# A depthwise convolution as 32x32 matrix tiles in place of 128x32 tiles, vector work and trips through DRAM

## The chip, the core and the metric

The kernel runs on one core of a Trainium2 chip. The core has a matrix engine (TensorE, "PE" in the profile; its weight loads are "PEld"), a vector engine (VectorE, "DVE"), an activation engine (ScalarE, "ACT"), a general engine (GpSimd, "POOL") and a queue engine (SyncE, "SP") that issues most DMAs. Each engine works through its own instructions in order and waits on semaphores for the others. Operands lie in SBUF (128 partitions); TensorE writes its sums to PSUM (eight banks of 512 fp32 numbers per partition). The metric is the time of one execution on the device in microseconds (us).

## What is computed

One step of a streaming encoder: a 512-frame prompt and 8 running streams of 16 new frames each, 640 frames of 1024 features. Layer 0 is a convolution module and a SwiGLU feed-forward block; layer 1 is chunked attention and a second feed-forward block. Only the convolution module concerns us:

```python
def conv_module(h, hist, g, w_pw1, b_pw1, w_dw, b_dw, ln_g, ln_b, w_pw2, b_pw2):
    a, gate = jnp.split(rms_norm(h, g) @ w_pw1 + b_pw1, 2, axis=-1)
    glu = a * jax.nn.sigmoid(gate)
    full = jnp.concatenate([hist.astype(glu.dtype), glu], axis=1)
    y = lax.conv_general_dilated(
        full, w_dw[:, None, :].astype(full.dtype), window_strides=(1,), padding="VALID",
        dimension_numbers=("NWC", "WIO", "NWC"), feature_group_count=D_MODEL) + b_dw
    y = jax.nn.silu(layer_norm(y, ln_g, ln_b))
    return h + y @ w_pw2 + b_pw2, full[:, -CONV_HIST:]
```

The convolution is depthwise and causal: each of the 1024 channels has its own filter of 31 taps over time, and 30 frames of history (zeros for the prompt, `cache_conv` for the streams) stand ahead of the new frames. The last 30 rows of `full` are outputs as well.

## The kernel before

Features lie on partitions: 1024 features are eight blocks (c = 0 to 7) of 128. Frames lie along the free dimension: first the 128 stream frames, then the 512 prompt frames, worked on as two groups of 320 (`GS`); group 0 holds all stream frames and the first 192 of the prompt. Every large product is made in three matmuls of high and low parts (`mm3`, lines L170 to L172, and `product`, L367), for which a weight tile is loaded as `raw` and split by ScalarE (`whi`, L150) and VectorE (`wlo`, L154). The two normalizations over features (`rms`, `conv_ln`) use small matmuls for the sums over partitions (L205) and for spreading the result back (L217).

In the convolution module each block c goes through these steps, written as letters in a list `PLAN` that a loop at the end of the module walks through (L817); a scheduler then places the instructions of each step on the engines, with raised priority for those inside `tc.high_priority`:

- W: load and split the block's weights of the first pointwise product, by DMAs on SyncE's queue (L139).
- a, b: the gated product (`glu`) for group 0 and group 1, 48 matmuls each; ScalarE takes the two sums out of PSUM (L596, L599), VectorE multiplies them (L603, the "gate").
- the depthwise convolution, in one of three ways:
  - d (`conv`): on VectorE, one multiply-add per tap (L676) into an accumulator in PSUM. Block 1's prompt and the stream frames of blocks 0, 1 and 2.
  - q (`conv_pool`): products on ScalarE (L686), sums on GpSimd (L689). The prompts of blocks 0 and 2.
  - k, X, Y, G, H: on TensorE, for blocks 3 to 7. The gate writes the frames into `g4` in four rows by time modulo four. That goes out to DRAM (`sc`, L631) and comes back as sixteen planes `x4` (`shift`, L643), in which a partition is one of four time shifts, one of eight channels and one of four time phases. `conv_w` (k, L696) builds 128x32 weight tiles on GpSimd from a table. `conv_pe` (G for group 0, H for group 1, L716) makes 64 matmuls for G and 32 for H, 128 rows by 32 columns each. VectorE adds the bias (`ev`, L721), the result goes out to DRAM (`ys`, L726) and back (L728) to be rearranged into `y`, and VectorE adds the three taps that the table does not hold, in three to six instructions (L739).
- n (`conv_ln`): LayerNorm and silu for one group, when `y` of all eight blocks is there. `LNO` is the order in which it takes up the blocks.
- w (`pw2`): the second pointwise product for one group, added to the residual `h` (L779).

PSUM before: the sums of products have four banks (`mm`), and the statistics and the VectorE convolution two tiles of two banks each (`w2`).

The order around the change is the list:

```python
LNO = ((0, 1, 3, 4, 5, 2, 6, 7), (0, 1, 2, 3, 4, 6, 7, 5))
PLAN = ("a0 y x1 b0 b1 q0 W2 W3 a2 b2 dp1s0 k3 a3 W4 b3 X3 q2 ds1s2 k4 a4 G3 k5 W5 b4 X4 a5 G4 k6 W6 a6 W7 a7 "
        "G5 Y7 k7 b6 W5 G6 k3 b7 W8 G7 n0 k4 H3 X6 k6 H4 X7 k7 b5 H6 X5 k5 H7 H5 s0 n1 w0 w1")
```

Of the kernel before, what the change touches and what calls it, by code (L numbers as in the profile page):

```python
# [15 lines left out]
P = 128  # L16
D = 1024
# [32 lines left out]
CVT = 4  # L50
C0, NC4 = 3, KT - 3
SG4 = SEG // 4 + 1
NS4, NP4 = NB * SG4, (HIST + T + 2) // 4
L4 = NS4 + NP4
KS, KA, KG = NB * SB // 4, 48, 80
WG, WH = NS4 + KA + 7, KG + 7
# [17 lines left out]
V_B4 = V_DW4 + NC4 * 128  # L74
# [4 lines left out]
def tile_trunk(ctx, tc, xT, vecs, hist, hist4, w_pw1, w_pw2, w_in0, w_out0, w_in1, w_out1,  # L79
# [7 lines left out]
    w2 = early.enter_context(tc.tile_pool(name="w2", bufs=2, space=PSUM))  # L87
# [4 lines left out]
    mm = tps.enter_context(tc.tile_pool(name="mm0", bufs=4, space=PSUM))  # L92
# [9 lines left out]
    def w2t():  # L102
        return w2.tile([P, 1024], F32, tag="w2", name=nm("w2"))
# [24 lines left out]
    def wsplit(src, k, n, parts=1, pool=0, cuts=1, gains=None):  # L128
# [6 lines left out]
        else:  # L135
            src = src if len(src.shape) == 2 else src.rearrange("p m c -> p (m c)")
            for i in range(cuts):
                a, b = sz * i // cuts, sz * (i + 1) // cuts
                nc.sync.dma_start(raw[:, a:b], src[:, a:b])  # L139
# [46 lines left out]
    def colmean(st, pieces, n, cut, tag, eng=nc.gpsimd, accp=None):  # L186
        nt = len(tiles(n))
        srcs = []
# [13 lines left out]
        for k, f in enumerate(srcs):  # L202
            s = f()
            for t, a in enumerate(tiles(n)):
                nc.tensor.matmul(st[:, 512 + t * w + k:513 + t * w + k], s[:, a:a + P],  # L205
                                 onec, start=True, stop=True)
        r = tp.tile([P, 4], F32, tag=tag, name=nm(tag))
        if w > 1:
            nc.vector.tensor_reduce(out=r[:, :nt],
                                    in_=st[:, 512:512 + nt * w].rearrange("p (t k) -> p t k", k=w),  # L210
                                    op=ALU.add, axis=mybir.AxisListType.X)
            return r, r[:, :nt]
        return r, st[:, 512:512 + nt]
# [329 lines left out]
    def load_hist(c0, c1):  # L543
        for c in range(c0, c1):
            if c < C0:
                nc.sync.dma_start(gs[:, c], hist[:, c])
            else:
                nc.sync.dma_start(g4[:, c - C0, :, 0:NS4], hist4[:, c - C0])
# [9 lines left out]
    g4 = cp.tile([P, NC4, 4, L4], F32, name="g4", tag="g4")  # L558
    for i in range(NC4):
        nc.gpsimd.memset(g4[:, i, :, NS4:NS4 + 8], 0.0)  # L560
        nc.gpsimd.memset(g4[:, i, 2:4, L4 - 1:L4], 0.0)
# [18 lines left out]
    def w4t():  # L580
        return cp.tile([P, 1024], F32, tag="w4", name=nm("w4"), bufs=2)

    def glu(c, g, wh, wl, mid=None):
# [10 lines left out]
        with tc.high_priority(offset=HP):  # L594
# [11 lines left out]
            ns = 0 if g else NB * SB  # L606
            o = HIST + g * NH - NB * SB * g
            if c < C0:
                if g == 0:
# [23 lines left out]
        if g == 0:  # L633
            if c < 7:
                shift(c, 0)
# [641 lines left out]
```

## Time and profile before

| | us |
|---|---|
| median of 3 runs | 1575.44 (1565.17 to 1576.24) |
| the profiled execution, its own time | 1576.21 |
| span of that execution in the trace | 1574.4 |
| TensorE busy in the span | 1473.0 (94%) |
| VectorE busy | 1019.5 (65%) |
| ScalarE busy | 671.0 (43%) |
| GpSimd busy | 241.4 (15%) |

All times below are microseconds from the start of the span unless they say ns. The convolution module and the entry to the feed-forward block take the first 307 us; the first pointwise product starts at 17.7, the first LayerNorm's sums are complete at 201.5, and the second pointwise product starts at 225.4. A line of a list of groups gives the source line, engine, operation, output and inputs, shapes and count, then busy us, mean ns of one, and the idle time of the engine ahead of them with what ended it. A line of a timeline gives start, length, and count; in brackets the idle time before it. "PEclk" or a number below 1 after the busy times is the share of full clock speed that TensorE was granted.

### The profile page before, as it was taken

Reading aid. Unit: us, or ns where it says so; the run is one execution under the profiler, and the core shown is the slowest. Engines: PE = TensorE matmul, PEld = TensorE weight load, DVE = VectorE, ACT = ScalarE, POOL = GpSimd, SP = SyncE. Lnnn points to the kernel's source line nnn. Section 1 sums busy time; section 2 is a strip of 40 time slices with the busy share of each in tenths; the row PEclk is TensorE's granted clock in tenths of the full one; section 3 lists DMA queues with packets and bytes.
Section 4 is the critical chain, followed back from the end, with each engine's and each line's share of the span. In section 5 each row is a group of like instructions: output and inputs, shape, how many; then the busy total and the mean of one; then the engine's idle time right before and its main releaser. Section 6 shows DMA issues by size and latency. Waiting matters only on the chain.

```text
span 1574.4 us, 27608 instructions
## 1 busy us (share of the span) xinstructions
PE 1473.0 (94%) x11282; PEld 1414.4 (90%) x11282; DVE 1019.5 (65%) x2020; ACT 671.0 (43%) x1281; POOL 241.4 (15%) x297
## 2 busy tenths in 40 slices
PE   5977668999999999999999999997999999999997
PEld 5977668999999999999988788975999999999996
DVE  6777565785666566658675767563694665575555
ACT  4663334453244244246554444443453254244233
POOL 4876622100000000003221112011000000000001
PEclk9988769899999999999999999997999999999998
DMA  7279653402222223213655445352112213222211
GB/s 236 75 157 190 142 103 107 134 27 81 81 81 89 81 72 108 81 54 99 218 170 192 155 160 201 122 189 67 55 48 88 81 58 105 81 74 88 81 54 67
DMA packets 89183, 171.29 MB, mean 109 GB/s; under 512 B 35552, under 2 KB 60128, under 8 KB 80224
## 3 DMA queue, kind: packets, MB, share of 16 engines
q1 hardware_dynamic: 88768, 169.01, 35.0%
q8 instruction: 88, 1.44, 0.4%
q10 hardware_dynamic: 288, 0.51, 0.1%
q14 instruction: 39, 0.32, 0.1%
HBM read 155.89 MB, written 13.62 MB: 108 GB/s over the span
## 4 chain that ended last, share of the span: by engine, by line
PE 78%; DVE 9%; DMA 6%; ACT 2%; POOL 2%; issue 2%; SPq 1%; POOLq 0%; DVEq 0%; ACTq 0%
PE mm L367 35%; PE mm L170 12%; PE mm L171 12%; PE mm L172 12%; DMA cache<-in_ck 2%; DVE wlo L154 1%; DMA ys<-ev 1%; PE w L1057 1%; DVE w L676 1%; PE am L1042 1%; DMA sc<-g 1%; POOL ca L689 1%; PE am L1025 1%; DVE g L603 1%; PE am L1088 1%
## 5 line engine op out<-in xcount | busy, mean ns | idle before, releaser
L367 PE MATMUL mm<-XH,wlo 128*128 128x320 f32 x736 | 228.8, 311 | 0.8 <-DVE wlo L325 0.8
L367 PE MATMUL mm<-XH,whi 128*128 128x320 f32 x736 | 227.5, 311 | 0.0
L367 PE MATMUL mm<-XL,whi 128*128 128x320 f32 x736 | 225.2, 309 | 0.0
L170 PE MATMUL mm<-xh,whi 128*128 128x320 f32 (+2 forms) x640 | 204.9, 323 | 11.3 <-ACT xh L159 5.3
L171 PE MATMUL mm<-xh,wlo 128*128 128x320 f32 (+2 forms) x640 | 203.7, 320 | 1.1 <-DVE wlo L154 1.1
L172 PE MATMUL mm<-xl,whi 128*128 128x320 f32 (+2 forms) x640 | 199.0, 317 | 0.4 <-DVE xl L160 0.4
L171 PE MATMUL mm<-hid,wlo 128*128 128x320 f32 (+2 forms) x560 | 171.8, 308 | 0.0
L172 PE MATMUL mm<-hid,whi 128*128 128x320 f32 (+2 forms) x560 | 169.3, 308 | 0.0
L170 PE MATMUL mm<-hid,whi 128*128 128x320 f32 (+2 forms) x560 | 167.7, 308 | 0.0
L324 ACT ACTIVATE whi<-raw 128x1536 fp32r<-128x1536 f32 (+2 forms) x90 | 100.9, 1149 | 119.6 <-PE mm L172 87.9
L325 DVE TENSOR_TENSOR wlo<-raw,whi 128x1536 fp32r<-128x1536 f32 (+2 forms) x90 | 118.6, 1342 | 39.9 <-ACT whi L324 39.8
L367 PEld LDWEIGHTS mm<-XH,wlo 128*128 128x128 f32 x736 | 139.2, 189 | 1.6 <-DVE wlo L325 1.6
L367 PEld LDWEIGHTS mm<-XH,whi 128*128 128x128 f32 x736 | 138.9, 189 | 0.0
L170 PEld LDWEIGHTS mm<-xh,whi 128*128 128x128 f32 x640 | 124.9, 196 | 14.8 <-ACT xh L159 6.4
L367 PEld LDWEIGHTS mm<-XL,whi 128*128 128x128 f32 x736 | 138.0, 188 | 0.0
L171 PEld LDWEIGHTS mm<-xh,wlo 128*128 128x128 f32 x640 | 125.4, 196 | 2.1 <-DVE wlo L154 1.6
L172 PEld LDWEIGHTS mm<-xl,whi 128*128 128x128 f32 x640 | 123.4, 194 | 1.9 <-issue 1.0
L367 PE MATMUL mm<-XH,vhi 128*128 128x320 f32 x368 | 114.7, 312 | 0.0
L367 PE MATMUL mm<-XL,vhi 128*128 128x320 f32 x368 | 113.8, 310 | 0.9 <-DVE XL L452 0.8
L367 PE MATMUL mm<-XH,vlo 128*128 128x320 f32 x368 | 114.4, 311 | 0.0
L171 PEld LDWEIGHTS mm<-hid,wlo 128*128 128x128 f32 x560 | 105.1, 188 | 0.0
L172 PEld LDWEIGHTS mm<-hid,whi 128*128 128x128 f32 x560 | 104.6, 188 | 0.0
(214 smaller groups left out, 3389.4 us busy)
## 6 DMA issues: line engine op xcount, KB each, us to landing
raw<-in_w_in SPq DMA_DIRECT2D x38, 1024.0 KB
cache<-in_ck SPq DMA_DIRECT2D x32, 512.0 KB
cache<-in_cv SPq DMA_DIRECT2D x32, 512.0 KB
raw<-in_w_pw SPq DMA_DIRECT2D x15, 1024.0 KB
raw<-in_w_out SPq DMA_DIRECT2D x18, 768.0 KB
raw<-in_w_kq SPq DMA_DIRECT2D x8, 1024.0 KB
raw<-in_w_in SPq DMA_DIRECT2D x12, 512.0 KB
x<-sc SPq DMA_DIRECT2D x20, 296.0 KB
```

The lines of the kernel that those rows point to most:

```text
L154: eng.tensor_tensor(out=lo[:, a:b], in0=raw[:, a:b], in1=hi[:, a:b].bitcast(F32), op=ALU.subtract)
L170: nc.tensor.matmul(ps, wh, xh, start=(i == 0), stop=False)
L171: nc.tensor.matmul(ps, wl, xh, start=False, stop=False)
L172: nc.tensor.matmul(ps, wh, xl, start=False, stop=(i == last))
L324: nc.scalar.activation(out=hi[:, a:b], in_=src, func=AF.Copy)
L325: nc.vector.tensor_tensor(out=lo[:, a:b], in0=src, in1=hi[:, a:b].bitcast(F32), op=ALU.subtract)
L367: nc.tensor.matmul(pt, wt, v[x][:, k, :], start=(first and k == i == 0), stop=(k == 3 and i == 2), skip_group_check=True)
L603: nc.vector.scalar_tensor_tensor(out=out, in0=f(t), scalar=1.0, in1=f(a), op0=ALU.add, op1=ALU.mult)
L676: nc.vector.scalar_tensor_tensor(out=dst, in0=src, scalar=wj, in1=dst, op0=ALU.mult, op1=ALU.add)
L689: nc.gpsimd.tensor_tensor(out=acc, in0=acc, in1=pr, op=ALU.add)
L1025: nc.tensor.transpose(tr[:, o:o + P], S[:, SOFF[i] + k * P:SOFF[i] + (k + 1) * P], ident)
L1042: nc.tensor.matmul(po[r, k * P:512], VT[:, 1 + k, v0:v0 + DH], PTs[hh][:, POFF[k]:POFF[k] + n], start=(k == 0), stop=(k == 3))
```

## The change

Six blocks (2 to 7) are convolved on TensorE instead of five, and no block on GpSimd; VectorE convolves blocks 0 and 1 whole, now into an SBUF tile `st`. The step q is gone.

The tiles are 32 rows by 32 columns. A row is one of eight channels and one of four time phases, a column one of the eight channels and one of four output phases. A filter of 31 taps then takes nine windows w of four frames (`NW = 9`), with all taps in the table, so that the three corrections of L739 are gone. Four row groups b and four column groups a make 16 tiles; each matmul has 80 columns of frames, the four row groups write to four banks (`pc`), and six results of 80 columns have room beside each other in a bank.

The gate of a TensorE block is one instruction per group (before: two to six). For group 0 it writes `gE`, a ring of three, in which the stream frames and twelve segments of the prompt lie in segments of twelve columns; GpSimd copies the parts that neighbouring prompt segments share, and the start of group 1's store `gB`. The shifted copies are four DMAs from SBUF to SBUF for each block and group, and the results go from `ev` to `y` in four DMAs from SBUF to SBUF. Nothing of this goes through DRAM. The channels within a block of `y` stand in another order, and the LayerNorm's parameters and the rows of the second pointwise weights are permuted on the host to match.

The weights of step W are loaded on ScalarE's queue instead of SyncE's. In PSUM the product sums have three banks instead of four, the statistics one tile of one bank, and `pc` four banks. Weight builds have three buffers instead of two.

```diff
-CVT = 4
-C0, NC4 = 3, KT - 3
+C0, NC4 = 2, KT - 2
+NW = 9
...
-LNO = ((0, 1, 3, 4, 5, 2, 6, 7), (0, 1, 2, 3, 4, 6, 7, 5))
-PLAN = ("a0 y x1 b0 b1 q0 W2 W3 a2 b2 dp1s0 k3 a3 W4 b3 X3 q2 ds1s2 k4 a4 G3 k5 W5 b4 X4 a5 G4 k6 W6 a6 W7 a7 "
-        "G5 Y7 k7 b6 W5 G6 k3 b7 W8 G7 n0 k4 H3 X6 k6 H4 X7 k7 b5 H6 X5 k5 H7 H5 s0 n1 w0 w1")
+LNO = ((0, 2, 3, 4, 1, 5, 6, 7), (0, 1, 2, 3, 4, 5, 6, 7))
+PLAN = ("a0 y x1 b0 b1 W2 W3 dp0s0 k2 k3 k4 a2 b2 X2 G2 k5 W4 a3 b3 X3 dp1s1 G3 k6 W5 a4 b4 X4 G4 k7 W6 a5 b5 G5 "
+        "k2 W7 a6 a7 G6 k3 b6 W8 G7 k4 n0 H2 X5 b7 k5 H3 X6 k6 H4 X7 k7 H5 H6 H7 s0 n1 w0 w1")
...
+    pcp = early.enter_context(tc.tile_pool(name="pcp", bufs=1, space=PSUM))
+    mm = tps.enter_context(tc.tile_pool(name="mm0", bufs=3, space=PSUM))
...
+            elif g == 0:
+                gate(ge(c)[:, :, :, 8:12].rearrange("p u s w -> p (u s) w"),
+                     lambda x: x[:, :n].rearrange("p (s m u) -> p u s m", m=4, u=4))
+                for j in (1, 2):
+                    nc.gpsimd.tensor_copy(ge(c)[:, :, NB + j:, 8 - 4 * j:12 - 4 * j],
+                                          ge(c)[:, :, NB:NSG - j, 8:12])
+                nc.gpsimd.tensor_copy(gB[:, c - C0, :, 0:8], ge(c)[:, :, NSG - 1, 4:12])
             else:
...
+                gate(gB[:, c - C0, :, 8:], lambda x: x[:, :n].rearrange("p (k u) -> p u k", u=4))
...
     def shift(c, g):
-        w = (WG, WH)[g] - 3
-        x4 = cp.tile([P, 16, w], F32, tag=f"x{g}", name=nm("x4"), bufs=2)
-        src = scs[c, g].rearrange("(z c) r w -> (c r) z w", c=8)
+        x4 = cp.tile([P, 4, (WG, WH)[g]], F32, tag=f"x{g}", name=nm("x4"), bufs=3)
+        src = gB[:, c - C0] if g else ge(c).rearrange("p u s w -> p u (s w)")
         for a in range(4):
-            nc.sync.dma_start(x4[32 * a:32 * a + 32], src[:, :, a:a + w])
+            nc.sync.dma_start(x4[:, a], src[32 * a:32 * a + 32])
...
     def conv(items):
-        st = w2t()
+        st = cp.tile([P, 1024], F32, tag="st", name=nm("st"))
...
+        for w in range(NW):
+            for a in range(4):
+                for b in range(4):
+                    r = slice(32 * b, 32 * b + 32)
...
+                    nc.tensor.matmul(pc[32 * a:32 * a + 32, b, o:o + KG],
+                                     w4[r, NW * a + w].rearrange("p c f -> p (c f)"), mv,
+                                     start=(w == 0), stop=(w == NW - 1), skip_group_check=True)
...
-            ys = dr.tile([P * 4, KG], F32, tag="ys", name=nm("ys"), bufs=4)
-            nc.sync.dma_start(ys.rearrange("(r p) k -> p r k", p=P), ev)
...
+            for b in range(4):
+                nc.sync.dma_start(y[g][32 * b:32 * b + 32, c, :], ev[:, b, :])
...
-            pws[c] = wsplit(w_pw1[c] if c < KT else w_pw2[0], 16, P)
+            pws[c] = wsplit(w_pw1[c] if c < KT else w_pw2[0], 16, P, q=nc.scalar)
```

More of the change, by code (lines that the diff above doesn't have):

```diff
@@ L86, in tile_trunk @@
     xp = early.enter_context(tc.tile_pool(name="xp", bufs=1))
-    w2 = early.enter_context(tc.tile_pool(name="w2", bufs=2, space=PSUM))
+    w2 = early.enter_context(tc.tile_pool(name="w2", bufs=1, space=PSUM))
+    tp2 = [512]
     uid = [0]
@@ L679, in conv @@
             to_y(c, NB * SB * part, dst.shape[-1], dst, func=AF.Copy)
-    def conv_pool(c):
-        acc = cp.tile([P, T], F32, tag="ca", name=nm("ca"))
-        for j in range(W):
-            wj = dcol(V_DW + c * W + j)
-            pr = acc if j == 0 else cp.tile([P, T], F32, tag="cvt", name=nm("cvt"), bufs=CVT)
-            nc.scalar.activation(out=pr, in_=taps(c, 1, j), func=AF.Identity, scale=wj,
-                                 **({} if j else {"bias": col(V_BDW, c)}))
-            if j:
-                nc.gpsimd.tensor_tensor(out=acc, in0=acc, in1=pr, op=ALU.add)
-        to_y(c, NB * SB, T, acc, func=AF.Copy)
@@ L818, in tile_trunk @@
         step(tok[0], tok[1:])
+    tp2[0] = 1024
     early.close()
```

154 lines of the change are left out of this document (59 added, 95 removed).

## The prediction

> **What bounds the kernel now.** I read the busy slices first, then a table by stage, then what TensorE waited for, then the instruction times of the convolution alone. The page (span, busy tenths in 40 slices of 39.4 us):
>
> ```profile
> span 1574.4 us, 27608 instructions
> PE   5977668999999999999999999997999999999997
> DVE  6777565785666566658675767563694665575555
> PEclk9988769899999999999999999997999999999998
> ```
>
> TensorE is full from slice 9 on; only the first eight slices, the convolution layer, show 5 to 7 tenths and a granted clock down to 0.6. So the change works where there is room. By stage (busy us and instructions of each engine, clock, DMA share, GB/s):
>
> ```profile
> 0.00:38.26 38.26, 21.74 (x121) 20.89 (x121) 23.27 (x45) 14.84 (x29) 19.23 (x45) 1.00 0.78 242
> 38.26:88.70 50.44, 49.89 (x336) 49.27 (x336) 40.51 (x77) 33.17 (x50) 41.49 (x31) 1.00 0.24 79
> 88.70:225.40 136.70, 89.53 (x1363) 86.29 (x1362) 90.79 (x195) 50.78 (x80) 81.72 (x77) 0.77 0.76 163
> 225.40:307.00 81.60, 73.13 (x462) 71.19 (x462) 56.14 (x85) 44.24 (x71) 17.68 (x16) 0.90 0.33 105
> 307.00:1574.40 1267.40, 1238.67 (x9002) 1186.80 (x9002) 808.80 (x1622) 527.93 (x1055) 81.31 (x130) 0.98 0.30 100
> ```
>
> Until 88.7 TensorE runs dense GLU matmuls: 336 in 50.44 us, 0.150 us each, 48 to a GLU step. Nine of the 16 GLU steps are done then (two before 38.26). From 88.7 to 225.4, where the second pointwise product starts, it idles 136.7 - 89.5 = 47.2 us. That is what can be won; from 307 on TensorE is full and the code is the same, so I book nothing there. The waits, and SyncE's own (engine, line waited for: us, times, longest):
>
> ```profile
> PE mm L716 <- DMA x<-sc: 31.8, 5, 8.1
> POOL w L696 <- PE mm L716: 34.2, 3, 21.2
> DVE y L739 <- DMA y<-ys: 31.9, 8, 9.9
> SPq L139 <- DVE wlo L154: 86.2, 9, 23.8
> ```
>
> The convolution's matmuls (L716) wait 31.8 us for their shifted copies, VectorE's corrections (L739) 31.9 us for y. Why those are late shows in the chain of work (first two rows, start and length): a hop out to DRAM took 9.08 us, and the hop back starts only then, 4.87 us for y, 2.14 in a quiet moment.
>
> ```profile
> 101.41 9.08 DMA sc<-g
> 111.48 4.87 DMA y<-ys
> 219.65 2.14 DMA y<-ys
> ```
>
> **The change, part by part.**
>
> *Matmuls.* Before: five channel blocks, 64 + 32 matmuls each, recorded as 960 pairs of weight load and matmul, so two pairs to a matmul. After: six blocks x two groups x 144 = 1728 matmuls, 3456 pairs, each of 32 rows by 32 columns and 80 wide. TensorE's timeline prices a pair (start, length of the run, count):
>
> ```profile
> 158.04 1.42 PE L716 MATMUL mm<-x,w 128*32 128x32 f32 x128
> 197.45 4.00 PE L205 MATMUL w<-onec,y 128*128 128x1 f32 x18
> 203.39 1.49 PE L217 MATMUL w<-ident,mst 128*128 128x128 f32 x6
> 204.81 1.45 PE L716 MATMUL mm<-x,w 128*32 128x80 f32 x72
> 212.02 2.36 PE L716 MATMUL mm<-x,w 128*32 128x80 f32 x64 [5.76 <-DMA x<-sc]
> 218.23 1.44 PE L205 MATMUL w<-onec,acc 128*128 128x1 f32 x6 [3.85 <-DVE acc L196]
> 221.49 1.65 PE L217 MATMUL w<-ident,rst 128*128 128x128 f32 x6 [1.81 <-POOL rst L245]
> ```
>
> Columns 32 and 48 wide at full clock: 1.42/128 = 11.1 ns a pair. Width 80: 1.45/72 = 20.1 ns, and 2.36/64 = 36.9 ns after a wait, at a low clock. These use four column groups of the array and all its rows. The new tiles use 16 places, four row groups beside four column groups; no row here shows row groups side by side. If they overlap fully, 20.1/4 = 5.0 ns; if not at all, 20.1 ns. I take 11 ns, the fastest issue any row shows: 3456 x 11 = 38.0 us, against 960 pairs in the sum above.
>
> The Trainium skill, "TensorE: Matmul & The Clock Gate", section "Wait — 56ns, not 53.3ns?", says that matmuls never start closer than about 25 ns, however narrow. By that the estimate is 86.4 us of convolution, 48 us more than mine, and no gain is left. The 11.1 ns row disagrees with it, so I keep it as a rival only.
>
> *TensorE's chain.* From 88.7: seven GLU steps, 336 x 0.150 = 50.4; convolution 38.0; the first LayerNorm's small matmuls (L205, L217 above) 4.0 + 1.5 + 1.4 + 1.7 = 8.6. Sum 97.0, so 185.7 at best. (A conv step ahead of 88.7 pushes GLU work behind it: the same sum.)
>
> *VectorE's chain.* Groups from the first 330 us (busy us, mean ns, idle before):
>
> ```profile
> L689 POOL TENSOR_TENSOR ca<-ca,cvt 128x512 f32<-128x512 f32 x60 | 89.2, 1487 | 16.0 <-ACT ca L686 6.1 <-ACT cvt L686 5.9
> L696 POOL TENSOR_TENSOR w<-i,dwv 128x256 f32<-128x256 f32 x40 | 29.2, 771 | 38.9 <-PE mm L716 34.2 <-DVE xl L160 4.5
> L676 DVE SCALAR_TENSOR_TENSOR w<-gall,dwv,w 128x128 f32<-128x128 f32 x90 | 26.7, 349 | 0.0
> L676 DVE SCALAR_TENSOR_TENSOR w<-gall,dwv,w 128x512 f32<-128x512 f32 x30 | 22.5, 749 | 0.0
> L739 DVE SCALAR_TENSOR_TENSOR y<-g,dwv,y 128x32 f32<-128x32 f32 (+2 forms) x45 | 17.8, 446 | 32.0 <-DMA y<-ys 31.9
> L721 DVE TENSOR_TENSOR ev<-mm,dwv 128x320 f32<-128x320 f32 x10 | 4.8, 487 | 10.7 <-DMA ys<-ev 9.6 <-PE mm L716 1.0
> L779 DVE SCALAR_TENSOR_TENSOR h<-mm,vec,h 128x320 f32<-128x320 f32 x16 | 12.5, 806 | 12.1 <-PE mm L172 12.0
> ```
>
> Gone: the 45 corrections L739 (17.8 us), and on GpSimd the two channel convolutions (89.2 us; on ScalarE their products). New on VectorE: both halves of channel blocks 0 and 1, 31 steps x 2 x (0.749 + 0.349) = 68.1 us. The gates become one instruction of 320 instead of two to six; I take L779's 0.806 us, also 320 with a stride. From the end of the second normalization (first row below) to the first LayerNorm VectorE needs: 68.1 of convolution; seven weight remainders x 2.28 = 16.0 (fourth and fifth rows below); eleven gates, 8.9, and 1.6 for blocks 0 and 1; six evictions x 0.487 = 2.9. Sum 97.5, so 143 without idling or contention.
>
> ```profile
> 44.07 1.40 DVE L160 TENSOR_TENSOR xl<-n,xh 128x320 fp32r<-128x320 f32 x2
> 162.19 3.06 DVE L603 SCALAR_TENSOR_TENSOR g<-t,t 128x160 f32<-128x160 f32 x2
> 198.47 0.78 DVE L603 SCALAR_TENSOR_TENSOR g<-t,t 128x160 f32<-128x160 f32 x2
> 166.57 3.35 DVE L154 TENSOR_TENSOR wlo<-raw,whi 128x2048 fp32r<-128x2048 f32 x1
> 184.02 2.28 DVE L154 TENSOR_TENSOR wlo<-raw,whi 128x2048 fp32r<-128x2048 f32 x1
> 201.49 0.18 DVE L209 TENSOR_REDUCE mst<-w 128x3 f32<-128x24 f32 x1 [2.24 <-PE w L205]
> 225.45 0.64 PE L170 MATMUL mm<-xh,whi 128*128 128x320 f32 x1 [2.31 <-ACT xh L159]
> ```
>
> Contention: the same two gates take 3.06 us while GpSimd convolves and 0.78 while it rests. The old accumulator lay in PSUM, and its steps kept 0.349 beside a busy GpSimd; the new one lies in SBUF, so its steps can be blocked too. GpSimd has in that time eight weight builds (k), 4 instructions of 288 elements, 0.771 x 288/256 = 0.87 each, 27.8 us, and 18 overlap copies, by size about 6 us. Between 0 and 34 us of it lands on VectorE; I take half, 17. Then 160, plus 4 for the column sums, plus the LayerNorm's 24 (the last two rows, 201.5 to 225.45): 188. The Trainium skill, "SBUF — State Buffer", section "SBUF: two separate sides", has this as an exclusive lock held for a whole instruction, between a GpSimd operation that reads SBUF and a VectorE one with two SBUF inputs. The gate rows agree; by it every collision counts and the estimate is nearer to the full 34, the second rival below.
>
> *DMA.* Per block and group four copies inside the chip, then four for y, replace out-and-back pairs. No on-chip copy is in the trace: its bounds are 2.14 us (quiet) and 9.08 us (sc). I take the quiet 2.14, since the copies have 128 rows and not 512, and put four issues of 0.4 us ahead. For the shifts the other group's GLU step (7.2 us) covers this. After the last tile (G7) nothing does: 0.5 + 1.6 + 2.1 = 4.2 us, on the path.
>
> *Queues and banks.* On GpSimd the overlap copies stand behind the weight builds, and these wait for a conv step to free a buffer (today 34.2 us in three waits). Now there are three buffers: the build for block 5 waits for step G2 alone, which by the new order comes before block 3's copies; if G2 were late, block 3's shift and G3 would be late behind it, one step of 3.2 us, which the GLU steps between cover. Block 5's history load shares a ring place with block 2, whose copies go out three blocks earlier: nothing. Weight loads go from SyncE's queue to ScalarE's:
>
> ```profile
> L139 SPq DMA_DIRECT2D raw<-in_w_pw x11: 332/358/433, 23.1 to 207.8; - x11
> ```
>
> Issuing is cheap (ns, least, median, most), but a load that waits for its buffer now holds up ScalarE's evictions, and three banks instead of four hold the GLU sums, so TensorE waits after one half step (3.6 us). ScalarE loses the products and has time: I book 2 us. One statistics bank instead of two costs nothing, since each spread is used up before the next sums.
>
> *Sum.* The two chains end at 185.7 and 188; the later, plus 4.2 and 2, is 194 against 225.4: 31 us. The 81.6 us behind it stay. The profiled execution's own time is 1576.21 (the median shown is 1575.44): 1576.2 - 31 = **1545**.
>
> **The rivals.**
> 1. *A pair costs more than 21 ns* (slower). Place: the twelve conv steps on TensorE. Its chain reaches today's 225.4 when 88.7 + 50.4 + 8.6 + 6.2 + 3.456 t = 225.4, t = 20.7 ns. The 36.9 ns row is a cold one, and small tiles may not lift the clock. Halfway between 20.1 and 36.9, 28.5 ns gives 98.5 us: 1576 + 27 = 1603. Against it: work before each conv step is dense. 0.13. The 25 ns of the page named above would give 1591, an estimate.
> 2. *VectorE is blocked by GpSimd* for the full 34 us: 17 more, 1562. For it the gate rows; against it that GpSimd loses 89 us. 0.14.
> 3. *Row groups don't overlap*: 20.1 ns, 69.5 us, chain end 223, 1574. 0.12.
> 4. *The hop isn't shorter* (the change doesn't do what it says): at 9.08 us, with 1.6 of issues and 1 of copies on GpSimd, a shift misses its cover of 7.2 by 4.5 us in six G steps, 27 us on TensorE's chain, 219: 1570. 0.04.
> 5. *ScalarE's queue stalls*: SyncE's nine waits for remainders averaged 9.6 us; 6 beyond the 3.6 us, seven times, 42 us, takes all back: 1587 at most. 0.05.
>
> **How the numbers follow.** The forecast has 0.52: 1528 (pair at 5 ns, no contention) to 1560. About 1% (16 us) is what a measurement of this kernel can tell from no change. Faster: 0.50 of the forecast, half of rival 2 and 0.03 of rivals 3 and 4, whose times scatter too: 0.60. Same: 0.02 and 0.07 left of the first two, 0.13 of rivals 3 and 4, 0.04 of rival 5: 0.26. Slower: rival 1 and the rest of 5, 0.14. Range 1524 to 1583: 0.06 below it and 0.14 above it are left out.
>
> **What would show it.** Right: the matmul group of the new conv at some 11 ns a pair (3.2 us a step); no wait for a shifted copy over 2 us; the second pointwise product starting near 194; everything behind unchanged. Wrong: conv steps over 6 us; clock under 0.8 in them; VectorE full with its two-channel convolution still running past 165; ScalarE waiting on weight loads.

## The result and the profile after

| | before | after |
|---|---|---|
| median of 4 runs each, us | 1572.37 (1565.17 to 1576.24) | 1632.33 (1628.29 to 1637.81) |
| ratio to before, 95% interval | | 1.039 [1.034, 1.044] |
| span of the profiled execution, us | 1574.4 | 1626.5 |

The changed kernel is slower by 60 us by the medians and 52 by the profiled executions, where 31 us less were forecast. The table by stage of the changed kernel (length; busy us and instructions of PE, PEld, DVE, ACT, POOL; clock; DMA share; GB/s) has the same cuts as before, and one more at 358, where the feed-forward block is now entered:

```profile
38.26:88.70 50.44, 41.83 (x531) 40.19 (x529) 44.04 (x69) 15.42 (x24) 13.42 (x17) 0.94 0.31 93
88.70:225.40 136.70, 107.89 (x2136) 102.04 (x2136) 58.75 (x100) 20.71 (x31) 33.70 (x39) 0.81 0.26 71
225.40:307.00 81.60, 63.57 (x1760) 59.32 (x1761) 29.89 (x49) 21.29 (x32) 16.47 (x22) 0.85 0.22 61
307.00:358.00 51.00, 40.43 (x258) 39.54 (x256) 31.05 (x44) 27.11 (x46) 14.15 (x13) 0.87 0.37 124
358.00:1626.50 1268.50, 1237.56 (x9020) 1186.95 (x9020) 816.18 (x1635) 531.88 (x1062) 81.53 (x130) 0.99 0.30 100
```

The last stage takes 1268.5 us against 1267.4: the whole loss lies ahead of it. What the change promised on its way it did: the DMA share of the third stage fell from 0.76 to 0.26, GpSimd from 81.7 to 33.7 us. Yet TensorE is busy 107.9 us there and still not done.

The groups of TensorE over the whole span say what took the place of the waits (busy us, mean ns | idle before, with what ended it). First before, then after:

```profile
L170 PE MATMUL mm<-xh,whi 128*128 128x320 f32 (+2 forms) x640 | 204.9, 323 | 11.3 <-ACT xh L159 5.3 <-DVE ev L721 5.2 <-ACT whi L142 0.5
L171 PE MATMUL mm<-xh,wlo 128*128 128x320 f32 (+2 forms) x640 | 203.7, 320 | 1.1 <-DVE wlo L154 1.1
L172 PE MATMUL mm<-xl,whi 128*128 128x320 f32 (+2 forms) x640 | 199.0, 317 | 0.4 <-DVE xl L160 0.4
L716 PE MATMUL mm<-x,w 128*32 128x32 f32 (+2 forms) x960 | 20.3, 261 | 34.1 <-DMA x<-sc 31.8 <-issue 2.3
```

```profile
L172 PE MATMUL mm<-xh,whi 128*128 128x320 f32 (+2 forms) x640 | 209.8, 329 | 13.4 <-ACT xh L161 12.0 <-ACT whi L144 0.7 <-ACT t L606 0.4
L173 PE MATMUL mm<-xh,wlo 128*128 128x320 f32 (+2 forms) x640 | 207.5, 325 | 3.3 <-issue 3.3
L174 PE MATMUL mm<-xl,whi 128*128 128x320 f32 (+2 forms) x640 | 203.7, 324 | 1.9 <-issue 1.0 <-DVE xl L162 0.9
L705 PE MATMUL pc<-x,w 32*32 32x80 f32 x3456 | 49.0, 255 | 41.6 <-issue 32.9 <-DVE st L674 8.4 <-DMA x<-gE 0.2
```

| TensorE, us | before | after | difference |
|---|---|---|---|
| wait for shifted copies | 31.8 | 0.2 | -31.6 |
| convolution busy | 20.3 | 49.0 | +28.7 |
| pauses put down to "issue" | 2.3 | 37.2 | +34.9 |
| dense products of three (the first three rows), busy | 607.6 | 621.0 | +13.4 |
| wait of one conv step (G3), put down to VectorE's `st` | 0 | 8.4 | +8.4 |
| waits for ScalarE's `xh` and VectorE's `ev` | 10.5 | 12.0 | +1.5 |

The sum is +55.3, the span grew by 52.1. So the wait that was to go went for the most part (for G3 see below), and nearly three quarters of what came instead are the pairs themselves: their own time and pauses that no semaphore explains. "Issue" is idle time for which the profile shows no releaser. TensorE's timeline shows its pattern; this is one conv step (start, length of the run, count, idle before), with the dense matmuls that follow:

```profile
142.41 2.00 PE L705 MATMUL pc<-x,w 32*32 32x80 f32 x157
146.01 1.62 PE L705 MATMUL pc<-x,w 32*32 32x80 f32 x128 [1.60 <-issue]
150.29 0.32 PE L705 MATMUL pc<-x,w 32*32 32x80 f32 x3 [2.65 <-issue]
150.98 0.47 PE L172 MATMUL mm<-xh,whi 128*128 128x320 f32 x1
151.25 0.47 PE L173 MATMUL mm<-xh,wlo 128*128 128x320 f32 x1
154.37 0.31 PE L174 MATMUL mm<-xl,whi 128*128 128x320 f32 x1
154.52 0.31 PE L172 MATMUL mm<-xh,whi 128*128 128x320 f32 x1
```

Inside a run a pair costs 12.7 ns (2.00/157 and 1.62/128; the granted clock was 1.00). But the step stops twice, and between the stops lie exactly 128 pairs, which is 256 instructions. The 288 pairs take 8.1 us, not 3.2. Behind the step the dense matmuls start 0.27 us apart and not 0.15, until about 154. The granted clock was 0.57 from 151.0 to 154.4 and 1.00 behind that: so behind the pauses time is lost to a lower clock, too.

Rows around the largest semaphore wait of a conv step, G3's: ScalarE's; VectorE's convolution and GpSimd's overlap copies for blocks 2 and 3, and those for block 4; the last shifted copy of block 3 in the chain of work; TensorE's.

```profile
95.29 1.22 ACT L652 ACTIVATE y<-st 128x192 f32<-128x192 f32 x2 [14.41 <-DVE st L674]
72.97 5.47 DVE L674 SCALAR_TENSOR_TENSOR st<-gall,dwv,st 128x512 f32<-128x512 f32 x7
73.11 1.57 POOL L623 COPY gE<-gE 128x176 f32<-128x176 f32 x2 [17.82 <-DVE gE L610]
100.68 6.56 DVE L674 SCALAR_TENSOR_TENSOR st<-gall,dwv,st 128x512 f32<-128x512 f32 x14
100.82 11.37 POOL L623 COPY gE<-gE 128x176 f32<-128x176 f32 x2 [6.10 <-DVE gE L610]
135.69 0.64 POOL L623 COPY gE<-gE 128x176 f32<-128x176 f32 x2 [7.83 <-DVE gE L610]
114.18 2.51 DMA x<-gE
114.92 1.02 PE L705 MATMUL pc<-x,w 32*32 32x80 f32 x16 [8.43 <-DVE st L674]
```

ScalarE's copy of VectorE's finished convolution waits 14.4 us, ahead of GLU evictions. Then the two overlap copies on GpSimd take 11.37 us (the first alone 11.04) while VectorE convolves beside them. They took 1.57 us for block 2, also beside VectorE's multiply-adds, and 0.64 for block 4, when VectorE was all but done; what made the one copy so much longer is not shown. The profile puts G3's wait down to `st`, but VectorE works on `st` all through it. What G3 needs are the shifted copies: GpSimd is done with the overlap at 112.2, the four DMAs are issued one after another from there, and the last lands at 116.7. G3's first 16 pairs at 114.9 are followed by a short wait for the next copy, and the chain of work runs from these copies to G3 as well. So the 8.4 us are a wait for shifted copies, too: 31.8 us before, 8.6 after.

So there were two theories. **Instructions:** TensorE eats small pairs faster than blocks of 256 instructions arrive, so a step runs at the pace of the supply. **Queues:** the chain ScalarE, gate, copies, DMAs is late, and the pauses only fill time in which TensorE would wait anyway.

### The profile page after: what moved, and what is told of

Read it like the earlier page. It is cut to its first block, busy times and chain, and to the rows that moved or that the text cites. A ratio compares the mean times of both kernels' runs of the same rounds, so it can differ in the third digit from the quotient of the medians.

```text
span 1626.5 us, 32437 instructions
## 1 busy us (share of the span) xinstructions
PE 1507.3 (93%) x13778; PEld 1442.9 (89%) x13778; DVE 1006.8 (62%) x1945; ACT 628.4 (39%) x1215; POOL 177.7 (11%) x256
## 3 DMA queue, kind: packets, MB, share of 16 engines
q1 hardware_dynamic: 69472, 151.42, 28.7%
## 4 chain that ended last, share of the span: by engine, by line
PE 87%; DVE 5%; issue 3%; DMA 2%; POOL 1%; ACT 1%; SPq 0%; DVEq 0%; POOLq 0%; ACTq 0%
PE mm L370 34%; PE mm L172 14%; PE mm L174 14%; PE mm L173 14%; PE pc L705 3%; PE w L208 1%; PE w L1031 1%; PE am L1016 1%; DVE st L674 1%; PE am L1062 1%; PE am L999 1%; DMA cache<-in_ck 1%; POOL gE L623 1%; PE w L220 1%; PE w L975 1%
## 5 line engine op out<-in xcount | busy, mean ns | idle before, releaser
L172 PE MATMUL mm<-xh,whi 128*128 128x320 f32 (+2 forms) x640 | 209.8, 329 | 13.4 <-ACT xh L161 12.0
L173 PE MATMUL mm<-xh,wlo 128*128 128x320 f32 (+2 forms) x640 | 207.5, 325 | 3.3 <-issue 3.3
L174 PE MATMUL mm<-xl,whi 128*128 128x320 f32 (+2 forms) x640 | 203.7, 324 | 1.9 <-issue 1.0
L172 PEld LDWEIGHTS mm<-xh,whi 128*128 128x128 f32 x640 | 128.6, 201 | 18.7 <-ACT xh L161 12.8
L174 PEld LDWEIGHTS mm<-xl,whi 128*128 128x128 f32 x640 | 127.1, 200 | 5.0 <-issue 2.6
L173 PEld LDWEIGHTS mm<-xh,wlo 128*128 128x128 f32 x640 | 128.7, 201 | 2.9 <-issue 2.6
L370 PE MATMUL mm<-XH,vhi 128*128 128x320 f32 x368 | 114.9, 312 | 0.0
L370 PE MATMUL mm<-XH,vlo 128*128 128x320 f32 x368 | 114.5, 311 | 0.0
```

Source lines behind the costliest of these rows:

```text
L172: nc.tensor.matmul(ps, wh, xh, start=(i == 0), stop=False)
L173: nc.tensor.matmul(ps, wl, xh, start=False, stop=False)
L174: nc.tensor.matmul(ps, wh, xl, start=False, stop=(i == last))
L370: nc.tensor.matmul(pt, wt, v[x][:, k, :], start=(first and k == i == 0), stop=(k == 3 and i == 2), skip_group_check=True)
```

## The experiments

Ratios are to the kernel before, timed beside each run on the same chip; brackets are 95% intervals. The runs were taken on several chips, so ratios compare better than times.

**The supply by itself.** To the kernel before, at its end, 1024 pairs of 32x32 tiles with 80 columns are added, 1024 with 320 columns, and 256 pairs of 128x128 tiles with 80 columns, all on data that is long there:

```diff
+        for n, o in ((80, 0), (320, 128)):
+            for w in range(32):
...
+                        nc.tensor.matmul(pq[32 * a:32 * a + 32, b, o:o + n], h[r, a, 0:32],
+                                         h[r, w % 8, 128:128 + n], start=True, stop=True,
...
+        for w in range(128):
+            nc.tensor.matmul(pq[:, w % 4, 0:80], h[:, 0, 0:P], h[:, w % 8, 128:208], start=True,
```

> The kernel before, with matmuls added behind its end that write nothing that is used: 512 matmuls (1024 pairs) of 32x32 tiles 80 wide in the order of the new conv step, 1024 pairs 320 wide, then 128 wide-array matmuls (256 pairs, 128x128, 80 wide). No data is loaded meanwhile. Theory (instruction supply): runs of 128 pairs with pauses between them for both widths, a run with its pause about 3.3 us, so 27 us for each 1024 pairs, and no pause in the wide ones; 1572 + 65 = 1637. Rival (the pauses come from waits on data, semaphores or DMA traffic): no pauses here, 13 us for the first 1024 pairs. Rival (the pair itself is slow): no pauses, but more than 20 ns from pair to pair.

It was run once: 1648.94, where 1637 was expected; a single run's total says little, and only the timeline is used here. TensorE's, at the end of that kernel:

```profile
1575.15 2.18 PE L1181 MATMUL pq<-h 32*32 32x80 f32 x128 [1.29 <-issue]
1578.62 2.18 PE L1181 MATMUL pq<-h 32*32 32x80 f32 x128 [1.29 <-issue]
1603.47 3.18 PE L1181 MATMUL pq<-h 32*32 32x320 f32 x128 [0.29 <-issue]
1606.94 3.18 PE L1181 MATMUL pq<-h 32*32 32x320 f32 x128 [0.29 <-issue]
1617.45 28.81 PE L1185 MATMUL pq<-h 128*128 128x80 f32 x256
```

A run of 128 pairs begins every 3.47 us, with 80 columns as with 320: four times the data changes the busy part and not the pace. Nor does the clock change it: it was 0.50 in the first two of these rows and 1.00 in the next two. Large tiles, 113 ns a pair, show no pause. The only DMA traffic in that stretch is the instruction queue's:

```profile
q8 instruction: 14, 0.23, 1.4%
```

0.23 MB in 14 packets is 16 KB a packet. So a long row of small pairs goes at 3.47/128 = 27 ns a pair, at the pace of the instruction blocks. The Trainium skill, "Runtime: NRT & Kernel Launch", section "Instruction fetch mechanics", says that the sequencer refills in 16 KiB blocks and that crossing one is "mostly hidden". The block size agrees; hidden it is not where a block lasts TensorE 1.6 to 2.2 us.

**The queues, one by one.** First the weight loads of step W back on SyncE's queue:

```diff
-            pws[c] = wsplit(w_pw1[c] if c < KT else w_pw2[0], 16, P, q=nc.scalar)
+            pws[c] = wsplit(w_pw1[c] if c < KT else w_pw2[0], 16, P)
```

> The changed kernel with one part undone: the weight loads of step W go through SyncE's queue again. Theory (instruction supply): TensorE's instructions come in blocks of 256, that is 128 pairs of weight load and matmul, and the twelve conv steps use a block up in 1.6 us where the next takes some 3.4; this edit doesn't touch that, so the 37 us of unexplained pauses around the conv matmuls stay. But ScalarE stood 7.2 us at the start behind a weight load that waited, and the first product of TensorE came at 24.8 instead of 17.7: that should go, 1632 - 7 = 1625. Rival (ScalarE's queue is the cause of the loss): 1590 or less. Second rival (it costs nothing, all is instruction supply): 1632 within 3.

1629.09, ratio 1.035 [1.033, 1.037]. The first dense product starts at 20.1 instead of 24.8, and the pauses at the conv line stay, at 31.3 us. But the time falls by 3 us only (by the medians), which the intervals don't tell from nothing: GpSimd's overlap copies for block 3 take 16.46 us here, and G3 waits 14.0 us instead of 8.4, now put down to the shifted copies. So this run doesn't price the queue change by itself.

Then the three overlap copies on ScalarE instead of GpSimd:

```diff
-                    nc.gpsimd.tensor_copy(ge(c)[:, :, NB + j:, 8 - 4 * j:12 - 4 * j],
-                                          ge(c)[:, :, NB:NSG - j, 8:12])
+                    nc.scalar.activation(out=ge(c)[:, :, NB + j:, 8 - 4 * j:12 - 4 * j],
+                                         in_=ge(c)[:, :, NB:NSG - j, 8:12], func=AF.Copy)
```

> The changed kernel with the three overlap copies of each block on ScalarE instead of GpSimd. One pair of copies took 11.4 us on GpSimd while VectorE convolved beside it, and step G3 waited 8.4 us for them. Theory (VectorE's steps with two SBUF operands hold GpSimd up): these 8.4 us go and smaller ones with them, 1632 - 9 = 1623; copies take under 1 us each. Instruction supply alone: the time goes nowhere, 1632 within 4, since TensorE would stand in its other pauses instead.

1632.15, ratio 1.037 [1.032, 1.041]: no gain. The copies do take 0.58 us for two, and the pauses at the conv line fall from 32.9 to 23.8. G3's wait falls to 3.5 us, but G4 now waits 4.4; all waits for shifted copies are 8.8. In the profiled execution the second pointwise product starts at 241.8 instead of 250.1; the stages behind it are longer and leave nothing of that, and why is not shown.

Then VectorE copies its own result into `y`, so that ScalarE does not wait for it:

```diff
-                nc.scalar.activation(
-                    out=y[g][:, c, :].rearrange("p (f k) -> p f k", f=4)[:, :, ku:kv],
-                    in_=perm(src[:, u - o:v - o]), **kw)
+                nc.vector.tensor_copy(
+                    y[g][:, c, :].rearrange("p (f k) -> p f k", f=4)[:, :, ku:kv],
+                    perm(src[:, u - o:v - o]))
```

> Undoes one suspected queue block in the changed kernel: the copies of VectorE's finished convolution (blocks 0 and 1) into y are made by VectorE itself, right behind its own convolution, instead of by ScalarE, so that ScalarE's GLU evictions no longer stand behind a copy that waits 14.41 us. Price: 6 copies on VectorE, 0.4 to 0.8 us each as on ScalarE, about 4 us. Theory A (the chain ScalarE, VectorE gate, copies, shift DMAs sets when G3 can start): a3's second eviction moves from 96.4 to about 86, gate 3 with it, G3's wait of 8.43 us goes, time 1632 less 6 to 10, about 1624. Rival B (TensorE's pauses for instructions are the bound and the wait on gE only overlaps them, or VectorE, which is busy 18 of 20 us there, delays the gate as much): the ScalarE wait goes, the time changes by less than 4 us.

1639.43, ratio 1.039 [1.036, 1.042]: no gain. ScalarE's wait for VectorE is gone, but it had cost next to nothing: ScalarE now waits 14.2 us for TensorE in its place and takes up the last sums of block 3's gate at 98.80 instead of 98.90. The gate follows at 100.68 (in the changed kernel 100.04), GpSimd's copies take 10.71 us, and G3 still waits 7.9. Last, VectorE's convolution of block 1 emitted later:

```diff
-... k5 W4 a3 b3 X3 dp1s1 G3 k6 ... a5 b5 G5
+... k5 W4 a3 b3 X3 G3 k6 ... a5 b5 G5 dp1s1
```

> Changes the order alone: VectorE's convolution of block 1 is emitted behind G5 instead of ahead of G3, so that it runs where VectorE was nearly idle (14 of 75 us busy from 150 to 225) and not between the gates of blocks 2 and 4. Theory A (G3's wait of 8.43 us is VectorE's load: the gate waits behind the convolution, and the GpSimd copies of 11.37 us for two are slow only because VectorE convolves beside them): the copies of block 3 take about 1.6 us for two, as elsewhere, and G3's wait is gone; time 1632 less 5 to 9. Rival B (the pauses for instructions take up the gain, or block 1 is late for the first LayerNorm): same time within 4 us.

1635.07, ratio 1.040 [1.037, 1.042]. This run tells nothing of its theory: the scheduler put the work where it had been (after the gate at 99.56 the next 14 instructions on VectorE are still that convolution), GpSimd's copies are as slow, and G3 waits 11.7 us:

```profile
100.36 11.35 POOL L623 COPY gE<-gE 128x176 f32<-128x176 f32 x2 [8.48 <-DVE gE L610]
```

**The pauses alone.** The windows of G2 to G6 and of H2 (32 pairs each) are handed out between the dense matmuls of the next GLU steps:

```diff
+            if spread and (i % 2 == 0 or i == last):
+                tick()
...
         for w in range(NW):
...
+            yield False
...
-            conv_pe(c, int(op == "H"))
+            todo.append(conv_pe(c, int(op == "H")))
```

> The changed kernel, same work and same instructions, but TensorE's order differs: steps G2 to G6 and H2 are not run as one run of 288 pairs; one window (32 pairs) stands after every second or so group of three wide matmuls of the next gated product. G7 and H3 to H7 stay as they are. Theory (instruction supply): the spread steps use a block of 256 instructions in about 4 us and find the next one there, so their pauses go, 3.1 us a step, and the low clock behind them, up to 1.5 us more: 6 steps, 1632 - 19 to 27 = 1605 to 1613. Rival (the small tiles are slow in themselves, or TensorE empties at each change of tile shape): no gain; at 0.1 to 0.2 us for each of 108 changes 1643 to 1654.

1626.62, ratio 1.032 [1.029, 1.036]: at most 6 us less, where 19 to 27 were expected, and the intervals overlap. Its timeline, one window among dense matmuls, and then G3:

```profile
84.66 0.31 PE L185 MATMUL mm<-xl,whi 128*128 128x320 f32 x1
84.89 0.42 PE L718 MATMUL pc<-x,w 32*32 32x80 f32 x32
85.25 0.42 PE L183 MATMUL mm<-xh,whi 128*128 128x320 f32 x1
85.50 0.31 PE L184 MATMUL mm<-xh,wlo 128*128 128x320 f32 x1
118.01 0.97 PE L718 MATMUL pc<-x,w 32*32 32x80 f32 x16 [18.75 <-DVE st L687]
```

The pauses at the conv line fell from 32.9 to 12.5 us: the same pairs, thinned out, don't starve. But G3's wait grew from 8.4 to 18.8 us (GpSimd's copies take 12.27 here). So both theories hold part of the stage, and half of what the pauses gave up went to that wait. A spread window also has a price: from the last dense start before it (84.66) to the second behind it (85.50) are 0.84 us, and not 2 x 0.15, so a window costs 0.54 us (0.36 from its first start to the next dense one, the rest at the two changes), and 108 windows would cost 58 us even with no pause at all.

**How much is the pairs?** In the changed kernel, five windows of nine, and one of nine:

```diff
-        for w in range(NW):
+        for w in range(5):
...
-                                     start=(w == 0), stop=(w == NW - 1), skip_group_check=True)
+                                     start=(w == 0), stop=(w == 4), skip_group_check=True)
```

> Leaves out four of the nine windows of every TensorE convolution step (the output of these six blocks is not the convolution): 160 pairs a step instead of 288, all else as in the changed kernel. Theory A (TensorE pauses because a step of small pairs eats instructions faster than blocks of 256 arrive; a step of 160 pairs fits what is already there): the issue pauses at the conv line and the dense product behind it fall from 37 us to below 10, far more than the 4 ninths of the pairs taken away; pairs still 12 to 13 ns each. Rival B (a small pair costs some 26 ns whatever stands around it): pauses fall in proportion, to about 20 us, and the time by 12 x 128 x 26 ns = 40 us. Under A time at pc about 43 us less, of which the wait on VectorE and ScalarE (G3) takes back up to 15: 1590 to 1605.

> Leaves out eight of the nine windows of every TensorE convolution step (32 pairs a step; six blocks of the output are not the convolution), all else as in the changed kernel: what the change would be worth if its products cost TensorE next to nothing. Theory A (the instruction supply and the pairs themselves make the loss): against five windows (1588.5) another 12 x 128 pairs at 12.6 ns go, 19 us, and the 13 us of pauses left there: about 1557 to 1570, just below before; VectorE's chain (98 us of convolution, gates behind it, copies on GpSimd) then sets the end and keeps it from the forecast 1545. Rival B (VectorE, ScalarE and the copies are the larger part of the loss): it stays at 1580 or above.

Five windows: 1588.52, ratio 1.007 [1.004, 1.009], just below what was expected. One window: 1542.25, ratio 0.980 [0.977, 0.984], lower than I expected. The conv groups of the two, each with its instruction queue (packets, MB):

```profile
L705 PE MATMUL pc<-x,w 32*32 32x80 f32 x1920 | 29.0, 258 | 24.4 <-DMA x<-gE 14.2 <-issue 10.0
q8 instruction: 96, 1.57, 0.4%
```

```profile
L705 PE MATMUL pc<-x,w 32*32 32x80 f32 x384 | 9.5, 267 | 16.0 <-DMA x<-gE 7.9 <-POOL w L684 3.2 <-DVE ev L710 2.6
q8 instruction: 84, 1.38, 0.4%
```

```profile
q8 instruction: 108, 1.77, 0.4%
```

The last row is the changed kernel's. Each 1536 pairs are twelve packets, 256 instructions each. All pauses together (conv line and the dense lines behind) are 37.2 us with nine windows, 12.9 with five and none with one. 4 ninths fewer pairs would have left 20.7 with five, so they fall by more than in proportion, as the instruction theory wants, though not below the 10 that I had expected. The time alone doesn't tell the theories apart: it falls by much the same in both steps, 43.8 us and then 46.3 by the medians, some 50 and 42 by the ratios. The pairs' own busy time falls by 20.0 and 19.5, the pauses by 24.3 and 12.9; the rest is not worked out. Over both steps a pair costs (1632.33 - 1542.25)/3072 = 29 ns of the kernel's time.

The queues are not gone with one window. GpSimd's copies for block 4 take 8.43 us, G4 waits 6.0 us for its shifted copies, and the waits at the conv line are 16.0 us, against 8.6 with nine windows (pauses put down to issue not counted). Yet this kernel is 33 us faster than before. So those waits don't make the loss, and the pairs with their pauses do:

```profile
169.70 0.18 DVE L212 TENSOR_REDUCE mst<-w 128x3 f32<-128x24 f32 x1 [3.42 <-PE w L208]
195.97 0.64 PE L172 MATMUL mm<-xh,whi 128*128 128x320 f32 x1 [1.70 <-ACT xh L161]
```

The LayerNorm's sums are complete at 169.7, and the second pointwise product starts at 196.0.

**Both at once.** Windows spread, overlap copies on ScalarE, results copied by VectorE, weights on SyncE:

> Both suspected causes taken away at once: the conv windows of G2 to G6 and H2 spread between the dense products (e4), the three overlap copies on ScalarE (e2), VectorE's finished convolution copied into y by VectorE (e6), the weights of W on SyncE (e1). Each of them alone gave 0 to 6 us. Theory A (two bounds in series: relieve one and the other takes its place): issue pauses below 15 us and no wait on gE or st above 5 us together, time 1632 less about 20 (pauses) less 8 to 14 (G3's wait) less 3 (start), 1590 to 1602. Rival B (VectorE alone is the bound up to its last convolution at 130 us): VectorE's convolution still ends at 130 or later and the time stays above 1615.

1611.76, ratio 1.022 [1.017, 1.026]; better than any part, less than expected: G3 still waits 7.8 us. Its gate stands behind VectorE's convolution until 96.2, over 10 us after ScalarE took out the last sums for it (85.3). Then all twelve steps are spread and the LayerNorm of group 1 moves into the second pointwise product of group 0:

```diff
...
+PLAN = ("a0 y x1 b0 b1 W2 W3 dp0s0 k2 k2 k3 a2 b2 X2 W4 G2 a3 H2 b3 X3 k3 W5 G3 a4 H3 b4 X4 k4 k4 W6 G4 a5 H4 b5 X5 "
+        "k5 W7 dp1s1 G5 a6 k6 G6 a7 k7 W8 G7 b6 X6 k5 k6 n0 H5 b7 X7 k7 H6 H7 u0 s0 n1 w0 w1")
...
```

(u0 is the first half of w0.)

> Keeps the changed kernel's convolution whole, and orders the work around its supply of instructions: e7 (spread windows, overlap copies on ScalarE, VectorE's results copied by VectorE, weights on SyncE), all twelve steps spread over dense products (five blocks' G and H between the GLU products, H6 and H7 in the second pointwise product), VectorE's convolution of block 1 behind b5, the LayerNorm of the second token group emitted half way through the second pointwise product. Theory A (two bounds, instruction supply and VectorE's order): issue pauses at conv and dense lines below 8 us (e7: 20.6), no wait on st, pw2's first product at about 205; 1612 less 12 less 8, less up to 5 more: 1585 to 1595. Rival B (the change of tile shape between dense and small tiles, about 0.1 us each way in e4, and the clock cost as much as the pauses): pauses go but dense products get longer, time 1600 to 1612.

1607.31, ratio 1.021 [1.019, 1.023]. That is in the range of the rival, and not by its mechanism: the pauses did not go, 20.5 us at the conv line are still put down to "issue". Here this label misleads: two pauses, 7.0 and 7.7 us, end 0.1 us behind a VectorE eviction `ev` of the step before. So next block 1's convolution is listed two steps later and gets a buffer that is free only after G4, which does move it:

```diff
-        "k5 W7 dp1s1 G5 a6 k6 ...
+        "k5 W7 G5 a6 dp1s1 k6 ...
...
-        st = cp.tile([P, 1024], F32, tag="st", name=nm("st"))
+        st = w4t() if items[0][0] else cp.tile([P, 1024], F32, tag="st", name=nm("st"))
```

> The spread version (e9, 1607) with block 1's convolution on VectorE made to come later by a dependence, its buffer being one of the three that the weight tiles use, freed by G4's products; its place in the order alone did not move it in the run before (there VectorE's work, its sequence and the 11.35 us copies were as in the changed kernel). Theory A (VectorE's load between 80 and 130 holds the gates and the evictions ev, and TensorE's two waits of 7.0 and 7.7 us in e9, which end just after an ev, are those): both waits below 2 us, time 1590 to 1598. Rival B (TensorE is full without them): within 4 us of 1607.

1595.63, ratio 1.014 [1.011, 1.017], the time expected. Of the two pauses 3.2 us are left, but the convolution now stands ahead of a later eviction, and a new pause of 8.1 us is there. VectorE's rows, then TensorE's:

```profile
140.48 20.71 DVE L687 SCALAR_TENSOR_TENSOR w<-gall,dwv,w 128x128 f32<-128x128 f32 x45
161.10 0.49 DVE L724 TENSOR_TENSOR ev<-pc,dwv 128x320 f32<-128x320 f32 x1
```

```profile
161.69 1.69 PE L718 MATMUL pc<-x,w 32*32 32x80 f32 x96 [8.09 <-issue]
```

The conv burst starts 0.10 us after the eviction ends. Moving the evictions to ScalarE tests whether that wait is VectorE's or the supply's:

```diff
-            nc.vector.tensor_tensor(
-                out=ev, in0=pc[:, :, o:o + KG],
...
+            for b in range(4):
+                nc.scalar.activation(out=ev[:, b, :], in_=pc[:, b, o:o + KG], func=AF.Identity,
+                                     bias=dwv[:, V_B4 + 4 * i + b:V_B4 + 4 * i + b + 1])
```

> e12 (1595.6) with the evictions ev taken off VectorE: ScalarE adds the bias in four activations of 80 columns a step. In e12 TensorE's two longest pauses, 3.21 and 8.09 us, are put down to issue, yet each ends 0.1 us after an ev that stood behind VectorE's convolution (ev at 90.89 and 161.10 for 0.49, conv bursts at 91.48 and 161.69). Theory A (those pauses are that queue, not instructions): both below 1 us, time 1595.6 less 8 to 11, 1584 to 1588, still above before because the pairs keep 54 us of TensorE against 20. Rival B (they are instruction supply): the pauses stay, the time too, within 3 us. In no case below before.

```profile
L718 PE MATMUL pc<-x,w 32*32 32x80 f32 x3456 | 54.8, 254 | 15.1 <-DMA x<-gE 9.1 <-issue 5.4 <-ACT ev L725 0.4
```

1593.86, ratio 1.014 [1.010, 1.017], as far as the time goes the rival's. The 3.2 and 8.1 us are gone from "issue", which is 5.4 in all, so they were VectorE's queue. The time did not follow: one wait for a shifted copy, 7.3 us ahead of the burst at 172.4, took the place. The best order found keeps the change 1.4% slower than before. What remains is mostly the pairs: 54.8 us busy against 20.3 before.

## Why the prediction was wrong

**The step that failed** is the first term of TensorE's chain: "I take 11 ns, the fastest issue any row shows: 3456 x 11 = 38.0 us". Measured were 49.0 us busy and 37.2 us of pauses, 86 us. I took the pace of one run of 128 pairs as that of all steps. Inside its runs a pair came near it (12.7 ns), but my row was no longer than one instruction block, and a step of 288 pairs is 576 instructions, more than two. At the pace of the blocks, 27 ns a pair, TensorE was left waiting for instructions. The sign I had named, conv steps over 6 us, is there: 8.1. The bounds I set (5.0 and 20.1 ns) were both on the work of the array; none was on the number of instructions, which the change takes from 960 pairs to 3456.

**A second term failed with it:** "The 81.6 us behind it stay." I had put all twelve conv steps ahead of the second pointwise product. In the changed kernel that product starts at 250.1 and not at 194, with only eight steps done; four run inside it, and from its start to 358.0 it takes 107.9 us. The 56 us in front and 26 behind are the whole error. From 358 on the code is the same and took the same time, as forecast.

**What agrees, and how far.** With the pairs nearly gone (one window) the LayerNorm's sums are complete at 169.7 and the second pointwise product starts at 196.0, where I had 160 + 4 + 4.2 + 2 = 170 and 194; the time is 1542 beside my 1545. The times agree, the path does not. I had VectorE busy without a gap, for 97.5 + 17 = 114.5 us. In that kernel it is busy for 91.3 of 116.6 us up to its last eviction ahead of those sums (the row has length, then PE, PEld, DVE, ACT, POOL):

```profile
46.60:163.20 116.60, 105.70 (x837) 101.00 (x836) 91.28 (x138) 31.58 (x46) 51.89 (x47) 0.93 0.38 107
```

Waits that I had not put in filled the rest, so the agreement is luck in part.

**What I had not put in.** I let the other group's GLU step cover the shifts, and let GpSimd's and VectorE's collisions fall on VectorE, 17 us of them. In the changed kernel VectorE's 120 multiply-adds took 74.1 us, 8.2 more than at my prices, and it was GpSimd that was held up: one copy of 11.04 us made G3 wait 8.4. The dense matmuls' 13.4 us more, at a lower clock, were not in the sum either. Neither makes the loss: with one window the queues are as bad, and the change gains.

**The rivals.** The first had the side and the price: from 20.7 ns a pair the change loses, and 29 ns is what it cost. It had the wrong reason (cold small tiles: the runs at 12.7 ns had a granted clock of 1.00) and a time 29 us too low, 1603. Its second pointwise product would have started at 252, near the measured 250.1, but by accident: it had all twelve steps ahead of that, where eight were, and nothing for G3's wait or the dense matmuls' clock. The 25 ns that the Trainium skill gives in "TensorE: Matmul & The Clock Gate", section "Wait — 56ns, not 53.3ns?", would have led to a total of 86.4 us, very near the measured 86; but as a floor between two starts it is contradicted by the runs at 12.7 ns. The number was good, the mechanism is another. The second rival (VectorE blocked by GpSimd) is refuted as put: VectorE's convolution ended by 136, not past 165, and the long copy of 11.04 us is GpSimd's. The third is refuted: 12.7 ns with 16 tiles is below the 20.1 ns of tiles that take all rows. In the fourth, the hop itself is refuted, for a shifted copy landed in 2.5 us; but one step did miss its cover, G3 by 8.4 us, for the copies on GpSimd ahead of it and not for the hop. The fifth is real at the start (the first dense product at 24.8 instead of 17.7); with the weights back on SyncE 4.7 of these 7.1 us went, and the time fell by 3, not by 42.

**Chances.** 0.14 for slower was too little. The row that should have raised it was in view: 128 pairs in one run is where the old kernel's conv steps end, so it could say nothing of longer ones.

## What to carry to other kernels

Before cutting a product into small tiles, count instructions as well as array time: find in a trace the longest run of such pairs without a pause, and don't extend its pace beyond its length. A wait that is removed on one engine is only worth what the next chain leaves: here no single repair gave more than 6 us, and all of them with a new order 38. A pause labelled as issue is two different things; compare its end with the ends of the other engines' instructions before believing in either. The same goes for a wait that is put down to a tile, like G3's to `st`.

## What the runs showed of the hardware

- TensorE got its instructions in blocks of 256 (16 KB in the instruction queue), one per 3.47 us or more in a long run of small pairs, at 80 and at 320 columns, at a granted clock of 0.50 and of 1.00: 27 ns a pair. In the changed kernel a run of 128 pairs and the pause behind it took 4.0 to 6.2 us; what makes it longer there is not shown. A first run of 129 to 234 pairs went through before the first pause.
- Sixteen 32x32 tiles on four row and four column groups do work side by side: 12.7 ns a pair with 80 columns, where tiles of 128 rows took 20.1, both at a granted clock of 1.00. At 0.50 it was 17.0 (2.18/128).
- A change from dense to small tiles and back cost about 0.1 us each way: in the spread version a conv window starts 0.23 us after the last dense start (84.66, 84.89), and behind it the second dense matmul starts 0.25 us after the first (85.25, 85.50), where 0.15 is usual.
- GpSimd's copy of 128x176 fp32 took 0.33 us with VectorE idle (at 159.7), and beside VectorE's multiply-adds with two SBUF operands 0.79 us once and 11.04 us another time. The Trainium skill, "SBUF — State Buffer", section "SBUF: two separate sides", describes a lock between two such operations; these rows agree with it, though not every such copy is held for long.
- After a conv step with pauses, dense matmuls started 0.27 us apart for about 3.4 us, at a granted clock of 0.57 on average, and then 0.15 again.
